# A Strassen-like down product: two half groups of inner tiles, or one over all sixteen

## The chip, the cores and the metric

The kernel runs on one core of a Trainium2 chip. The metric is the device time of one execution in microseconds, and the number compared is the median of several runs.

## The reference

A trunk of two layers on 512 tokens of width 1024. Each layer is a SwiGLU half step, a token mixing (three kinds of attention with gates), and a second SwiGLU half step, with RMS norms before and after each:

```
def _swiglu(t, w_gate, w_up, w_down):
    return (jax.nn.silu(t @ w_gate) * (t @ w_up)) @ w_down

for l in range(DEPTH):
    f = _swiglu(_rmsnorm(h, ffn1_pre_g[l]), ffn1_w_gate[l], ffn1_w_up[l], ffn1_w_down[l])
    h = h + 0.5 * _rmsnorm(f, ffn1_post_g[l])
    ...                                        # token mixing
    f = _swiglu(_rmsnorm(h, ffn2_pre_g[l]), ffn2_w_gate[l], ffn2_w_up[l], ffn2_w_down[l])
    h = h + 0.5 * _rmsnorm(f, ffn2_post_g[l])
```

The inner width D_FF is 2816, that is 22 tiles of 128. So there are four SwiGLUs in a run. Their names in the kernel are a0, c0, a1 and c1; the profile leaves the digit out, so that pda stands for the down product's banks in a0 and a1, and pdc for those in c0 and c1.

## The kernel before

All products run in a split float32 form. Each operand x is cast by ScalarE to a rounded high part (`split`, line 179), VectorE takes the difference as the low part (line 180), and `mm3` (lines 205 to 207) issues three matmuls: high by high, high by low, low by high. In the down product the names of the parts are wh_da and wl_da for the weights, aha and ala for the left factor.

In each SwiGLU the first 16 of the 22 inner tiles go through a seven-product scheme on blocks of two by two (Strassen's, in Winograd's form). Products 0 and 1 add up to one block of the result; the other products are formed from sums and differences of blocks. For the down product, the 16 inner tiles are taken as two half groups of 8 tiles (`ci` 0 and 1; FC is 8, NC is 2). Each half group is a two by two scheme of its own: the left factor's blocks are 256 tokens by 4 inner tiles, the weight's blocks are 4 inner tiles by 512 columns. One product (ci, n) has 4 inner tiles, two tiles of 128 tokens (`e`), and three matmuls each, so 24 matmuls of 512 columns. The last 6 inner tiles (16 to 21) are done plainly: their gate and up columns come in pairs of tiles (18 and 20 here), and `down` multiplies them at the end.

The order of the jobs is written out by hand. `PLAN` (lines 1636 to 1642) weaves the down products, two at a time, between half jobs of the gate and up columns: ("g", 18, 0) is the first half of gate pair 18 (one tile of the pair, 24 matmuls) and ("g", 18, 1) the second; both use the same weights, which are loaded for the first and freed by the second. A `Queue` holds the jobs. When a job begins, the units (weight blocks) of the following jobs are loaded ahead, at least four of them. A unit is fetched by SyncE into a ring buffer ("raw" or "o"), then split into a wh and a wl buffer. The compiler's scheduler then sets the order on each engine.

The buffers that matter, by tag (line 101): four wh and four wl (split weights), two raw and, for the down product, two of the eight o buffers as the fetching ring; further o buffers hold kept weight blocks ("bt", two for each half group, needed from product 2 to product 6) and the hidden tiles 18 to 21; six v buffers hold the left factor's high and low parts and its running sum ("as", from product 2 to product 5); two "k" and two "tri" buffers hold the hidden rows (hr). Four PSUM banks have the tag z.

`products` makes the units of a half group and yields its seven jobs. `product` runs one: it makes the next product's left factor (`first_factor`), opens banks for products 0, 1 and 2, runs the matmuls, and evicts. Product 3, 5 and 6 go on accumulating in the banks of product 0, product 4 in those of product 2 (`SUM`, line 599). `TO` (line 600) says to which quarter of the result a product's bank is evicted, f32 tiles `dst.fs` (fa and fc in the profile). In the first half group, ScalarE copies (lines 875, 878) and VectorE adds (lines 876, 880); in the second half group everything is added by VectorE (line 880), but for product 1's bank, which starts from a ScalarE copy of what is there already (line 856).

`BlockUnit.load` makes the weight's sums and differences with VectorE (line 327). Product 4 uses the raw block of product 3 (`inherits`).

Of the kernel before, what the change touches and what calls it, by code (L numbers as in the profile page):

```python
# [9 lines left out]
F32 = mybir.dt.float32  # L10
# [3 lines left out]
ALU = mybir.AluOpType  # L14
# [3 lines left out]
P = 128  # L18
# [4 lines left out]
def kernel(  # L23
# [38 lines left out]
    nc = tc.nc  # L62
    _, S, D = x.shape
# [11 lines left out]
    FC = 8  # L75
    NC = 2
# [26 lines left out]
    def stile(shape, tag, name, dt=F32R):  # L103
        return sb.tile(shape, dt, tag=tag, bufs=BUFS[tag], name=name)
# [4 lines left out]
    def pbank(tag, name):  # L109
        return ps.tile([P, S], F32, tag=tag, bufs=4, name=name)  # L110
# [65 lines left out]
    def split(h_ap, l_ap, src, scale=None, later=False):  # L176

        if scale is None:
            both = [nc.scalar.copy(h_ap, src)]  # L179
            make = lambda: nc.vector.tensor_tensor(l_ap, src, h_ap.bitcast(F32), ALU.subtract)  # L180
        else:
            both = [nc.scalar.activation(h_ap, src, AF.Copy, scale=scale)]  # L182
            make = lambda: nc.vector.scalar_tensor_tensor(l_ap, src, scale, h_ap.bitcast(F32), ALU.mult, ALU.subtract)  # L183
        if later:
            return make
        both.append(make())
        if Q.pinned:
            for ins in both:
                tc.keep_in_program_order(ins)
# [279 lines left out]
    HF = (slice(0, S), slice(S, D))  # L469
# [129 lines left out]
    SUM = (0, 1, 2, 0, 2, 0, 0)  # L599
# [3 lines left out]
    def ffn(l, src, wg, wu, wd, dst, name, spare, parked, plan, aside=None):  # L603
# [6 lines left out]
        hid, st = {}, {}  # L610
# [116 lines left out]
        def beside(gen, steps, every):  # L727

            for i, us_ in enumerate(gen):
                if i % every == every - 1:  # L730
                    next(steps, None)
                yield us_
# [58 lines left out]
        def turn(tag):  # L791

            nm, g, r = st.pop("turn", (None, None, None))
            if nm is None:
                return
            g = g.rearrange("p f q -> p (f q)")
            for b in range(2):
                pt = pbank(tag, f"ht{nm}_{b}")
                for f in range(2):
                    for e in range(2):  # L800
                        nc.tensor.transpose(pt[:, (2 * f + e) * P:(2 * f + e + 1) * P],
                                            g[:, e * S + (2 * b + f) * P:][:, :P], ident[:])
                nc.scalar.copy(r[:, 2 * b:2 * b + 2], pt[:].rearrange("p (f q) -> p f q", f=2))
                yield 0.4

        def token_products(ci, up):

            w, nm = (wu if up else wg)[l, :, ci * FC * P:(ci + 1) * FC * P], f"{'gu'[up]}{name}_{ci}"
            keep = Keep(lambda k0: stile([P, 2, S], "o", f"t{nm}_{k0}", F32)[:])
            places, had = itertools.cycle(("raw", "o", "o")), {}  # L810
            for n in ORDER:
                uns = [BlockUnit(n, w, ND // 2, k, 2, S, keep, f"{nm}_{n}_{k}", n in (2, 4) or next(places))
                       for k in range(0, ND // 2, 2)]
                if n in (2, 4):
                    for un, of in zip(uns, had[n - 2 + (n == 4)]):
                        un.inherits(of)
                had[n] = uns
                run = lambda n=n, uns=uns: token_product(ci, up, n, uns)
                early = ci == 0 and not up and n in ORDER[:4]
                yield uns, (lambda run=run: beside(run(), itertools.islice(st["some"], 1), 2)) if early else run  # L820
# [4 lines left out]
        def first_factor(ci, n):  # L825

            a = lambda i, j: hr[2 * ci + j][:, :, HALVES[i]]
            nm = f"{name}_{ci}_{n}"
            h, l = (stile([P, FC // 2, S // 2], "v", f"a{x}{nm}")[:] for x in "hl")
            if n == 2:  # L830
                st["s", ci] = stile([P, FC // 2, S // 2], "v", f"as{nm}", F32)[:]
            s = st.get(("s", ci))
            if n == 2:
                nc.vector.tensor_tensor(s, a(1, 0), a(1, 1), ALU.add)
            elif n == 3:
                nc.vector.tensor_tensor(s, s, a(0, 0), ALU.subtract)
            elif n == 4:
                nc.vector.tensor_tensor(s, a(0, 1), s, ALU.subtract)
            elif n == 5:
                nc.vector.tensor_tensor(s, a(0, 0), a(1, 0), ALU.subtract)  # L840
            src = (a(0, 0), a(0, 1), s, s, s, s, a(1, 1))[n]
            split(h, l, src)
            st["a", ci, n] = h, l

        def product(ci, n, uns):
            if n == 0 and ci == 0:
                RINGS["o"] = 2
                dst.begin()
            if n < 6:
                first_factor(ci, n + 1)  # L850
            if n in (0, 1, 2):
                st["b", SUM[n]] = [pbank("z", f"pd{name}_{ci}_{n}_{e}") for e in range(2)]
            pts = st["b", SUM[n]]
            if n == 1 and ci:
                for e in range(2):
                    nc.scalar.copy(pts[e][:], dst.fs[e][:, HF[0]])
            h, l = st["a", ci, n]
            opens, ends = n in (0, 2) or (n == 1 and not ci), n in (1, 4, 6)
            for un in uns:
                for k in range(un.nk):  # L860
                    kk = un.k0 + k
                    for e in range(2):
                        c = slice(e * P, (e + 1) * P)
                        mm3(pts[e][:], h[:, kk, c], l[:, kk, c], un.h[:, k], un.l[:, k], opens and kk == 0,
                            ends and kk == FC // 2 - 1, free=True)
                        yield 3 * S * PE_US
                    if kk == FC // 2 - 2:
                        yield from turn("mm")
            if n == 0:
                return  # L870
            i, hf = TO[n]
            for e in range(2):
                f = dst.fs[2 * i + e][:, HF[hf]]
                if n == 1:
                    nc.scalar.copy(f, st["b", 0][e][:])
                    nc.vector.tensor_tensor(f, f, pts[e][:], ALU.add)
                elif ci == 0 and n in (2, 3, 6):
                    nc.scalar.copy(f, pts[e][:])
                else:
                    nc.vector.tensor_tensor(f, f, pts[e][:], ALU.add)  # L880

        def products(ci):

            keep = Keep(lambda k0: stile([P, 2, S], "o", f"bt{name}_{ci}_{k0}", F32)[:])
            w = wd[l, ci * FC * P:(ci + 1) * FC * P]
            for n in range(7):
                uns = [BlockUnit(n, w, FC // 2, k, 2, S, keep, f"d{name}_{ci}_{n}_{k}", ("raw", "o")[k // 2])
                       for k in range(0, FC // 2, 2)]
                if n == 4:
                    for un, of in zip(uns, had):  # L890
                        un.inherits(of)
                had = uns
                yield uns, (lambda n=n, uns=uns: product(ci, n, uns))

        marks, made = {}, {}

# [15 lines left out]
        def queue(what):  # L912
            kind, n = what[0], what[1]
            if kind in "gu":
                if n not in made:
                    made[n] = plain(n)
                ms = (what[2],) if what[-1] in (0, 1) and len(what) == 3 else range(2)
                uns = made[n][kind == "u"]
                run = (lambda: gates(n, uns, ms)) if kind == "g" else (lambda: ups(n, uns, ms))
                Q.add(uns if ms[0] == 0 else [], run)  # L920
            elif kind == "a":
                Q.add([], lambda: iter(first_factor(n, 0) or ()))
            elif kind == "m":
                if name == "a0":
                    Q.add([], mem_stats)
            else:
                if what not in made:
                    made[what] = products(n) if kind == "d" else token_products(n, kind == "U")
                for one in made[what]:
                    Q.add(*one)  # L930
                    break

        first_pair()
        for what in plan:
            queue(what)
# [698 lines left out]
            yield ("pe", 0.9)  # L1634

    PLAN = 7 * [("G", 0)] + [("m", 0)] + 7 * [("U", 0)] + 7 * [("G", 1)] + 6 * [("U", 1)] + [("a", 0), ("U", 1)]
    downs = iter(6 * [("d", 0)] + [("a", 1), ("d", 0)] + 7 * [("d", 1)])
    for f in (18, 20):
        for kind in "gu":
            for m in range(2):  # L1640
# [57 lines left out]
```

## Time and profile before

| | |
|---|---|
| median of 3 runs | 2399.95 us (2398.45 to 2400.62) |
| the profiled execution | 2400.15 us; span on the core 2398.4 us |
| TensorE, busy share of the span | 99% (11975 matmuls) |
| weight loads (PEld) | 84% |
| VectorE (DVE) | 78% |
| ScalarE (ACT) | 58% |
| granted TensorE clock, mean | 0.997 |
| bytes moved | 338.22 MB, mean 141 GB/s |

Matmuls are pipelined and their ends are modelled, so a share of 99% on TensorE does not yet say that it works at its peak. A row of a group gives the line, engine, operation, output and inputs, the count, then busy us, mean ns of one, and the engine's idle time before it with what ended it.

### The profile page before, as it was taken

Reading aid. Unit: us, or ns where it says so; the run is one execution under the profiler, and the core shown is the slowest. Engines: PE = TensorE matmul, PEld = TensorE weight load, DVE = VectorE, ACT = ScalarE, POOL = GpSimd, SP = SyncE. Lnnn points to the kernel's source line nnn. Section 1 sums busy time; section 2 is a strip of 40 time slices with the busy share of each in tenths; the row PEclk is TensorE's granted clock in tenths of the full one; section 3 lists DMA queues with packets and bytes.
Section 4 is the critical chain, followed back from the end, with each engine's and each line's share of the span. In section 5 each row is a group of like instructions: output and inputs, shape, how many; then the busy total and the mean of one; then the engine's idle time right before and its main releaser. Section 6 shows DMA issues by size and latency. Waiting matters only on the chain.

```text
span 2398.4 us, 31561 instructions
## 1 busy us (share of the span) xinstructions
PE 2375.6 (99%) x11975; PEld 2009.8 (84%) x11975; DVE 1862.4 (78%) x2462; ACT 1392.5 (58%) x2201; POOL 78.4 (3%) x134
## 2 busy tenths in 40 slices
PE   9999999999999999999999999999999999999998
PEld 7788889888888888888888888888888888888887
DVE  8878877577777789788788788766667777887885
ACT  6655565576656555555655554655666664655554
POOL 1000000000111000000000000000001100000000
PEclk9999999999999999999999999999999999999999
DMA  5654454222323555544645554532323235555444
GB/s 200 187 150 158 141 194 140 80 82 78 88 80 99 192 181 170 150 150 158 210 138 170 149 175 162 188 107 71 97 71 97 71 122 191 164 182 149 154 139 155
DMA packets 232171, 338.22 MB, mean 141 GB/s; under 512 B 10682, under 2 KB 125394, under 8 KB 232020
## 3 DMA queue, kind: packets, MB, share of 16 engines
q1 hardware_dynamic: 231924, 336.18, 44.3%
q8 instruction: 94, 1.54, 0.3%
q14 instruction: 57, 0.47, 0.1%
q0 software_dynamic: 96, 0.03, 0.0%
HBM read 319.39 MB, written 16.78 MB: 140 GB/s over the span
## 4 chain that ended last, share of the span: by engine, by line
PE 94%; DVE 3%; DMA 1%; ACT 1%; issue 1%; POOL 0%; DVEq 0%; SPq 0%; ACTq 0%
PE pg L206 4%; PE pg L205 4%; PE pg L207 4%; PE pda L206 3%; PE pda L207 3%; PE pda L205 3%; PE pdc L206 3%; PE pdc L207 2%; PE pdc L205 2%; PE pb L207 2%; PE pb L206 2%; PE pb L205 2%; PE pk L205 1%; PE pk L206 1%; PE pk L207 1%; PE pwo L206 1%
## 5 line engine op out<-in xcount | busy, mean ns | idle before, releaser
L205 PE MATMUL pg<-us_a,wh_wg 128*128 128x512 f32 x384 | 150.8, 393 | 0.0
L206 PE MATMUL pg<-us_a,wh_wg 128*128 128x512 f32 x384 | 149.6, 390 | 0.0
L207 PE MATMUL pg<-us_a,wl_wg 128*128 128x512 f32 x384 | 149.6, 390 | 0.0
L206 PE MATMUL pdc<-wl_dc,ahc 128*128 128x512 f32 x224 | 87.6, 391 | 0.1
L206 PE MATMUL pda<-wl_da,aha 128*128 128x512 f32 x224 | 87.6, 391 | 0.0
L205 PE MATMUL pda<-wh_da,aha 128*128 128x512 f32 x224 | 87.4, 390 | 0.0
L205 PE MATMUL pdc<-wh_dc,ahc 128*128 128x512 f32 x224 | 87.4, 390 | 0.0
L207 PE MATMUL pdc<-wh_dc,alc 128*128 128x512 f32 x224 | 87.2, 389 | 0.0
L207 PE MATMUL pda<-wh_da,ala 128*128 128x512 f32 x224 | 87.2, 389 | 0.0
L207 PEld LDWEIGHTS pg<-us_a,wl_wg 128*128 128x128 f32 x384 | 72.1, 188 | 15.2
L205 PEld LDWEIGHTS pg<-us_a,wh_wg 128*128 128x128 f32 x384 | 72.1, 188 | 14.1
L206 PEld LDWEIGHTS pg<-us_a,wh_wg 128*128 128x128 f32 x384 | 72.2, 188 | 14.0
L180 DVE TENSOR_TENSOR wl_dc<-raw_dc,wh_dc 128x1024 fp32r<-128x1024 f32 x50 | 61.2, 1224 | 29.1 <-ACT wh_dc L179 28.5
L180 DVE TENSOR_TENSOR wl_da<-raw_da,wh_da 128x1024 fp32r<-128x1024 f32 x50 | 61.2, 1224 | 22.0 <-ACT wh_da L179 21.7
L179 ACT CAST wh_dc<-raw_dc 128x1024 fp32r<-128x1024 f32 x50 | 52.7, 1054 | 43.8 <-PE pdc L207 14.9
L179 ACT CAST wh_da<-raw_da 128x1024 fp32r<-128x1024 f32 x50 | 52.7, 1054 | 38.7 <-PE pda L207 14.5
L183 DVE SCALAR_TENSOR_TENSOR wl_wg<-raw_wg,wh_wg 128x1024 fp32r<-128x1024 f32 x48 | 58.4, 1221 | 20.4 <-ACT wh_wg L182 20.1
L179 ACT CAST wh_uc<-raw_uc 128x1024 fp32r<-128x1024 f32 x44 | 46.3, 1053 | 41.9 <-PE pwc1u L207 10.3
L182 ACT ACTIVATE wh_wg<-raw_wg 128x1024 fp32r<-128x1024 f32 x48 | 50.6, 1057 | 28.0 <-PE pv L1089 12.6
L179 ACT CAST wh_ua<-raw_ua 128x1024 fp32r<-128x1024 f32 x44 | 46.2, 1052 | 34.5 <-PE pwa1u L207 10.3
L180 DVE TENSOR_TENSOR wl_uc<-raw_uc,wh_uc 128x1024 fp32r<-128x1024 f32 x44 | 53.7, 1221 | 13.0 <-ACT wh_uc L179 12.9
L180 DVE TENSOR_TENSOR wl_ua<-raw_ua,wh_ua 128x1024 fp32r<-128x1024 f32 x44 | 53.6, 1220 | 10.2 <-ACT wh_ua L179 10.2
(654 smaller groups left out, 8028.8 us busy)
## 6 DMA issues: line engine op xcount, KB each, us to landing
raw_da<-in_ffn_w_down_dram SPq DMA_DIRECT2D x66, 512.0 KB, 4.5
raw_dc<-in_ffn_w_down_dram SPq DMA_DIRECT2D x66, 512.0 KB, 4.9
raw_ga<-in_ffn_w_gate_dram SPq DMA_DIRECT2D x52, 512.0 KB, 3.8
raw_ua<-in_ffn_w_up_dram SPq DMA_DIRECT2D x52, 512.0 KB, 3.9
raw_gc<-in_ffn_w_gate_dram SPq DMA_DIRECT2D x52, 512.0 KB, 3.7
raw_uc<-in_ffn_w_up_dram SPq DMA_DIRECT2D x52, 512.0 KB, 3.7
raw_wg<-in_w_gate_dram SPq DMA_DIRECT2D x48, 512.0 KB, 3.5
raw_wo<-in_w_out_dram SPq DMA_DIRECT2D x24, 512.0 KB, 3.6
```

The source lines that it names most:

```text
L179: both = [nc.scalar.copy(h_ap, src)]
L180: make = lambda: nc.vector.tensor_tensor(l_ap, src, h_ap.bitcast(F32), ALU.subtract)
L182: both = [nc.scalar.activation(h_ap, src, AF.Copy, scale=scale)]
L183: make = lambda: nc.vector.scalar_tensor_tensor(l_ap, src, scale, h_ap.bitcast(F32), ALU.mult, ALU.subtract)
L205: nc.tensor.matmul(pt, lh, rh, start=start, stop=False, skip_group_check=free)
L206: nc.tensor.matmul(pt, lh, rl, start=False, stop=False, skip_group_check=free)
L207: nc.tensor.matmul(pt, ll, rh, start=False, stop=stop, skip_group_check=free)
```

## The change

The two half groups are merged. One list, `DOWN`, gives the order of all 14 products: for each n both half groups in turn, but products 3 and 4 of one half group stay together, since 4 uses 3's raw block. The banks are opened only in the first half group and evicted only after the second, so each of the seven products accumulates over all sixteen inner tiles in PSUM. After product (1,0) the second bank starts from a ScalarE copy of the first bank, and product 1 accumulates on it. `products` makes the units of both half groups with two sets of kept blocks. In `PLAN` 14 equal entries take the place of the two groups' entries; the separate job that made the second group's first factor is gone.

```diff
+        DOWN = [(ci, n) for ns in ((0,), (1,), (2,), (3, 4), (5,), (6,)) for ci in range(NC) for n in ns]
+
-        def product(ci, n, uns):
-            if n == 0 and ci == 0:
+        def product(at, uns):
+            ci, n = DOWN[at]
+            first, last = ci == 0, ci == NC - 1
+            if at == 0:
                 RINGS["o"] = 2
                 dst.begin()
-            if n < 6:
-                first_factor(ci, n + 1)
-            if n in (0, 1, 2):
-                st["b", SUM[n]] = [pbank("z", f"pd{name}_{ci}_{n}_{e}") for e in range(2)]
+            if at + 1 < len(DOWN):
+                first_factor(*DOWN[at + 1])
+            if first and n in (0, 2):
+                st["b", SUM[n]] = [pbank("z", f"pd{name}_{n}_{e}") for e in range(2)]
             pts = st["b", SUM[n]]
-            if n == 1 and ci:
-                for e in range(2):
-                    nc.scalar.copy(pts[e][:], dst.fs[e][:, HF[0]])
-            h, l = st["a", ci, n]
-            opens, ends = n in (0, 2) or (n == 1 and not ci), n in (1, 4, 6)
+            h, l = st.pop(("a", ci, n))
+            opens, ends = first and n in (0, 2), last and n in (1, 4, 6)
             for un in uns:
...
+            if not last:
+                return
             if n == 0:
+                st["b", 1] = [pbank("z", f"pd{name}_1_{e}") for e in range(2)]
+                for e in range(2):
+                    nc.scalar.copy(st["b", 1][e][:], pts[e][:])
                 return
             i, hf = TO[n]
             for e in range(2):
                 f = dst.fs[2 * i + e][:, HF[hf]]
-                if n == 1:
-                    nc.scalar.copy(f, st["b", 0][e][:])
+                if n in (4, 5):
                     nc.vector.tensor_tensor(f, f, pts[e][:], ALU.add)
-                elif ci == 0 and n in (2, 3, 6):
+                else:
                     nc.scalar.copy(f, pts[e][:])
-                else:
-                    nc.vector.tensor_tensor(f, f, pts[e][:], ALU.add)
...
+        def products():
+            keep = [Keep(lambda k0, ci=ci: stile([P, 2, S], "o", f"bt{name}_{ci}_{k0}", F32)[:]) for ci in range(NC)]
+            had = {}
+            for at, (ci, n) in enumerate(DOWN):
+                w = wd[l, ci * FC * P:(ci + 1) * FC * P]
+                uns = [BlockUnit(n, w, FC // 2, k, 2, S, keep[ci], f"d{name}_{ci}_{n}_{k}", ("raw", "o")[k // 2])
                        for k in range(0, FC // 2, 2)]
                 if n == 4:
-                    for un, of in zip(uns, had):
+                    for un, of in zip(uns, had[ci, 3]):
                         un.inherits(of)
...
-    downs = iter(6 * [("d", 0)] + [("a", 1), ("d", 0)] + 7 * [("d", 1)])
+    downs = iter(14 * [("d", 0)])
```

More of the change, by code (lines that the diff above doesn't have):

```diff
@@ L873, in product @@
                 f = dst.fs[2 * i + e][:, HF[hf]]
-                if n == 1:
-                    nc.scalar.copy(f, st["b", 0][e][:])
+                if n in (4, 5):
                     nc.vector.tensor_tensor(f, f, pts[e][:], ALU.add)
-                elif ci == 0 and n in (2, 3, 6):
+                else:
                     nc.scalar.copy(f, pts[e][:])
-                else:
[L880 to L887, printed above, removed]
+        def products():
[4 more added lines that the diff above has]
+                uns = [BlockUnit(n, w, FC // 2, k, 2, S, keep[ci], f"d{name}_{ci}_{n}_{k}", ("raw", "o")[k // 2])
                        for k in range(0, FC // 2, 2)]
                 if n == 4:
-                    for un, of in zip(uns, had):
+                    for un, of in zip(uns, had[ci, 3]):
                         un.inherits(of)
-                had = uns
-                yield uns, (lambda n=n, uns=uns: product(ci, n, uns))
+                had[ci, n] = uns
+                yield uns, (lambda at=at, uns=uns: product(at, uns))
         marks, made = {}, {}
@@ L927, in queue @@
                 if what not in made:
-                    made[what] = products(n) if kind == "d" else token_products(n, kind == "U")
+                    made[what] = products() if kind == "d" else token_products(n, kind == "U")
                 for one in made[what]:
```

## The prediction

> **What bounds the kernel now.** I read the page's first part, then its chain, then TensorE's own waits, then the four stretches in which the changed code runs.
>
> ```profile
> span 2398.4 us, 31561 instructions
> PE 2375.6 (99%) x11975; PEld 2009.8 (84%) x11975; DVE 1862.4 (78%) x2462; ACT 1392.5 (58%) x2201; POOL 78.4 (3%) x134
> ...
> PE 94%; DVE 3%; DMA 1%; ACT 1%; issue 1%; POOL 0%; DVEq 0%; SPq 0%; ACTq 0%
> ```
>
> TensorE is busy for 99% of the span, and 94% of the chain that ended last is its work. "Busy" is modelled for matmuls, so I look for idle time instead. The view of waits, for TensorE (engine, line, what it waited for: us in total, times, longest):
>
> ```profile
> PE pfl L1283 <- DVE fl L1334: 9.0, 2, 4.5
> PE warm L1558 <- DVE warm L1650: 1.3, 1, 1.3
> PE pwa0g L207 <- DVE ula L180: 1.1, 1, 1.1
> ...
> PE pga L654 <- ACT w_ga L179: 0.2, 1, 0.2
> ```
>
> These are four of thirteen rows. None of the thirteen names pda or pdc, the banks of the down product. The four stretches with these products (one for each SwiGLU), by windows:
>
> ```profile
> core 0: us, PE busy (x) PEld busy (x) DVE busy (x) ACT busy (x) POOL busy (x), PEclk, DMA share, GB/s
> 200.20:321.40 121.20, 121.20 (x538) 99.72 (x536) 100.44 (x99) 61.76 (x72) 0.00 (x0) 1.00 0.55 182
> ...
> sum 485.60, PE 485.52 PEld 400.19 DVE 398.94 ACT 248.23 POOL 0.00; mean PE 121.38 PEld 100.05 DVE 99.73 ACT 62.06 POOL 0.00
> ```
>
> In such a stretch stand 14 products and 8 half jobs of the gate and up columns (18 to 21) that the plan weaves between them, each of 24 matmuls. TensorE is busy for 121.20 of 121.20 us, at full clock (1.00); 121.20 over 22 jobs is 5.5 us a job (the 8 transposes at the start are in it). VectorE is busy for 100.44 us, 83%, ScalarE for half, the DMA engines for 55%. So this stage is TensorE's, and taking work off VectorE saves time only where VectorE's lateness is seen by TensorE. Where that is, the weight loads show, in the views of the tiles pda and pdc (what their engine waited for: us, times):
>
> ```profile
>   DVE wl_da L180: 1.3, 4
> ...
>   DVE wl_dc L180: 1.4, 4
> ```
>
> Eight waits, 2.7 us in all, two in each stretch. One of them, from the timeline (start, us, engine, operation, and in brackets the idle time before):
>
> ```profile
> 217.63 0.39 PE L205 MATMUL pda<-wh_da,aha 128*128 128x512 f32 x1
> 217.86 0.39 PE L206 MATMUL pda<-wl_da,aha 128*128 128x512 f32 x1
> 219.92 2.35 DVE L327 TENSOR_TENSOR raw_da<-bta,raw_da 128x1024 f32<-128x1024 f32 x2
> 220.59 1.06 ACT L179 CAST wh_da<-bta 128x1024 fp32r<-128x1024 f32 x1 [2.17 <-PE pda L207]
> 222.19 1.22 DVE L180 TENSOR_TENSOR wl_da<-bta,wh_da 128x1024 fp32r<-128x1024 f32 x1
> 223.46 0.19 PEld L206 LDWEIGHTS pda<-wl_da,aha 128*128 128x128 f32 x1 [0.42 <-DVE wl_da L180]
> ```
>
> At 217.63 product 2 of the first half group starts; at about 223.1, 24 matmuls later, product 3. Weights lie in four wh and four wl buffers. Between the two halves of a gate (or up) pair, its own weights hold two of each, so the products in between share the other two. Product 3's first split must wait until product 2 has used its first pair of tiles: ScalarE waits for TensorE until 220.59, casts for 1.06 us, VectorE comes to it at 222.19, after the block sums of 219.92, and is done at 223.41; the load of the low part runs at 223.46. That is the second product between the two halves of a gate: (0,3) and (1,3) here, which is twice per stretch, as counted. This is the only place where the stage touches TensorE.
>
> **The change part by part.**
>
> *What goes.* The evictions of the second half group, and what joined the groups:
>
> ```profile
> L880 DVE TENSOR_TENSOR fa<-fa,pda x28: 679/681/687, 239.4 to 1506.1; 128x512 f32<-128x512 f32 x28
> L878 ACT COPY fa<-pda x12: 576/585/589, 222.6 to 1447.1; 128x512 f32<-128x512 f32 x12
> L875 ACT COPY fa<-pda x8: 572/584/589, 206.3 to 1457.9; 128x512 f32<-128x512 f32 x8
> L876 DVE TENSOR_TENSOR fa<-fa,pda x8: 680/684/689, 211.7 to 1465.7; 128x512 f32<-128x512 f32 x8
> ...
> L856 ACT COPY pda<-fa 128x512 f32<-128x512 f32 x2 | 1.2, 579 | 0.0
> ```
>
> Counts for pda cover two stretches (L856: one), pdc is the same. VectorE has 14 + 4 = 18 additions in a stretch now, and keeps 4 (products 4 and 5): 14 go, 14 x 0.681 = 9.5 us a stretch, 38 us in all. ScalarE has 6 + 4 + 2 = 12 copies and keeps 10 (two from the first bank into the second, and eight evictions): 2 x 0.58 = 1.2 us a stretch. TensorE keeps every matmul, 14 x 24 a stretch. On the path: nothing. No row says that TensorE waited for an eviction; each bank is next used after at least one other job of 5.5 us, which covers two evictions (2 x 0.68). VectorE falls from 100.4 to 90.9 of 121.2 us.
>
> *What is added: one wait.* The second bank now gets its start by two ScalarE copies out of the first, after product (1,0) has ended; 2 x 0.58 = 1.2 us. The half gate job of 5.5 us lies between (1,0) and (0,1), which needs that bank: cost nothing; without that cover 1.2 us x 4 = 4.7 us. Queued behind these copies on ScalarE are the casts of weights for (0,1) and (1,1), with a job's time to spare.
>
> *What moves: the order.* Two products stand between jobs as before, but now they are (0,0)(1,0), gate 18 first half, (0,1)(1,1), gate 18 second half, (0,2)(1,2), up 18 first half, (0,3)(0,4), up 18 second half, (1,3)(1,4), gate 20 first half, (0,5)(1,5), gate 20 second half, (0,6)(1,6), up 20. The pairs that stand between two halves are now (0,1)(1,1), (0,3)(0,4) and (0,5)(1,5): three second products per stretch, (1,1), (0,4), (1,5), where there were two. (Before, up 18 and up 20 had a single product between their halves, which shares its buffers with nobody.) So 12 waits instead of 8. The trace does not show the new three. From below each is 0 (product 4 has its block in place from product 3, and 1 takes it raw, so neither stands behind a block sum as 3 does): then the 2.7 us are gained. From above each stands behind one more whole VectorE instruction:
>
> ```profile
> L180 DVE TENSOR_TENSOR ala<-asa,aha 128x1024 fp32r<-128x1024 f32 x16 | 19.5, 1221 | 2.5 <-PE pda L206 2.4
> ```
>
> 12 x 1.22 = 14.7 us, less the 2.7 that go: +12.0 us. I take today's mean, 2.7 / 8 = 0.34 us: 12 x 0.34 = 4.05, so +1.35 us. It is the nearest row, the same wait of the same weights.
>
> *Buffers.* Two running sums of the left factor live at once instead of one: with two factors' high and low parts that fills the six v buffers exactly, where one was spare. A factor for the next product can then be split only when the product before the present one has ended. In each pair the second product's factor has a half job and the first product in front of it, some 11 us, for at most three instructions (sum, cast, low part, about 3.5 us): nothing, and up to 1 us for each of 14 if VectorE is late. Four kept weight blocks live at once instead of two; with two ring buffers and the first two hidden tiles they fill the eight o buffers: nothing.
>
> *Transfers.* They are the same in number and size, but product 2's doubled loads now come twice in a row: 8 x 0.512 MB = 4.2 MB, at the stage's 182 GB/s 23 us. They start when (0,1)'s raw blocks have been split, during (1,0), and (1,2) starts five jobs later, 27 us. Hidden, with little to spare at that rate; product 3 and 5 now wait for a raw buffer that a gate's split frees a little over two jobs ahead, as product 2 did before with twice the bytes, and product 2 shows no wait on TensorE. The rows for transfers in section 6 give 4.5 us to landing:
>
> ```profile
> raw_da<-in_ffn_w_down_dram SPq DMA_DIRECT2D x66, 512.0 KB, 4.5
> ```
>
> *The sum.* Evictions 0, the new copy 0, order +1.35, buffers 0, transfers 0: +1.35 us. The profiled execution took 2400.15 us (span 2398.4 and 1.75 around it), so its like would take 2401.5; it lies 0.2 us above the median of the three runs, 2399.95, so I say **2401.3 us**. About 0.2%, 4.8 us, is what a measurement of this kernel can tell from no change, so this is "the same".
>
> **A rule against the row.** The weight loads' groups (busy us, mean ns, idle before them):
>
> ```profile
> L205 PEld LDWEIGHTS pg<-us_a,wh_wg 128*128 128x128 f32 x384 | 72.1, 188 | 14.1
> ...
> L206 PEld LDWEIGHTS pda<-wl_da,aha 128*128 128x128 f32 x224 | 42.1, 188 | 9.9 <-DVE wl_da L180 1.3
> ...
> L205 PEld LDWEIGHTS pda<-wh_da,aha 128*128 128x128 f32 x224 | 42.0, 188 | 8.8
> ```
>
> Before each load lie 8.8 us / 224 = 39 ns in the down product and 14.1 / 384 = 37 ns in the mixing gates, where nothing of this kind is evicted. So the 39 ns belong to the load itself, and only the 1.3 us with a releaser can be won. The Trainium skill, "Perfetto Trace Analysis", section "Identifying the Most-Contended Engine", says that matmul occupancy does not measure the distance to the roofline, and that the busy share of LDWEIGHTS does. By that rule the stage is at 100.05 of 121.38 us, and up to 4 x 21.3 = 85 us could still go; by the rows the sum stays at +1.35 us.
>
> **The rivals.**
>
> *Slower, VectorE late at the twelve places.* In (1,5) the block sums and the sum of the left factor stand ahead of the low part, as in the lines shown. If the fixed order of VectorE's queue puts one more 1.22 us instruction ahead at all of them, +12.0 us: 2412. It decides from a mean wait of (4.8 + 2.7) / 12 = 0.63 us, about twice today's. For it: VectorE still at 75%, four of the heavy products, (0,5)(1,5)(0,6)(1,6), now in a row. Against it: 9.5 us less work, and (1,1) and (0,4) need no block sum. 0.16.
>
> *Slower, SyncE's queue.* One transfer held back the others while it waited for a v buffer:
>
> ```profile
> SPq L1026 <- PE pda L207: 5.2, 1, 5.2
> ```
>
> That cost nothing. If fuller buffers bring one such wait into each stretch, and half of it reaches TensorE, 4 x 2.6 = +10.4 us: 2410. 0.07.
>
> *A little faster.* All waits go: 2399.95 - 2.7 = 2397.25, which is still within 0.2%. 0.08.
>
> *Clearly faster.* Either the stage has room after all: the 1.3 + 1.4 us are all that its own rows give, so this would need the 38 us of VectorE to be on the path, 2362: 0.02. (The rule of the Trainium skill above is on the side of this rival; the equal 37 and 39 ns speak against it.) Or the order of VectorE's queue shifts further on, and the 9.0 us of waits for fl go: 2391, 0.07; nothing in the change touches that code.
>
> That the change doesn't do what it says is not open: the additions are plainly gone from the code.
>
> **How the numbers follow.** Forecast 0.60, and the little gain 0.08, give "same" 0.68; slower 0.16 + 0.07 = 0.23; faster 0.02 + 0.07 = 0.09. The likeliest case by itself runs from 2397 to 2403. The range reaches up to just under the first slower rival, 2411, and down past the little gain by the spread of the runs, to 2396: left out are the clear gain, 0.09, and the upper part of the slower rivals, about 0.08.
>
> **What would show it.** The additions of line 880 fall from 56 to 16, VectorE's busy time in a stretch from 100 to about 91 us, and TensorE's stays at 121. The waits of weight loads for wl_da and wl_dc become 12, at (1,1), (0,4) and (1,5), with some 4 us in sum. No row of TensorE's waits names pd, fa or fc. Wrong would be: a wait of TensorE for ScalarE's copies into the second bank, for the left factor's low part, or for weights that a transfer brought late; or a stretch that is over 1 us longer than 121.4 us.

## The result and the profile after

The merged kernel takes 2407.91 us (median of 6 runs, 2407.06 to 2409.55) against 2400.28 us for the kernel before (6 runs, 2398.12 to 2400.86): 7.6 us more, ratio 1.0035 with a 95% interval of 1.0022 to 1.0048. That is slower by more than the 0.2% of the prediction, and inside its range.

First the page and the chain of waits of the kernel after:

```profile
span 2405.3 us, 31523 instructions
PE 2377.2 (99%) x11975; PEld 2009.5 (84%) x11975; DVE 1828.1 (76%) x2406; ACT 1387.5 (58%) x2193; POOL 78.3 (3%) x134
...
PE 88%; DVE 5%; DMA 4%; ACT 2%; issue 1%; DVEq 0%; SPq 0%; ACTq 0%
```

VectorE has 56 instructions and 34 us less, ScalarE 8 copies less, TensorE the same 11975 matmuls. But TensorE's part of the chain fell from 94% to 88%; VectorE and the DMA engines, which were at 3% and 1%, have 5% and 4%. TensorE's view of waits has two new rows for the down products, directly under the old first one:

```profile
PE pfl L1287 <- DVE fl L1338: 8.7, 2, 4.4
PE pda L206 <- DVE wl_da L180: 3.5, 4, 1.5
PE pdc L206 <- DVE wl_dc L180: 1.6, 2, 0.8
```

The four down stretches (windows; columns as before):

```profile
200.10:322.87 122.77, 121.34 (x537) 99.40 (x535) 91.57 (x85) 60.17 (x69) 0.00 (x0) 1.00 0.49 167
1049.00:1171.30 122.30, 121.52 (x538) 99.54 (x537) 90.29 (x83) 61.21 (x70) 0.00 (x0) 1.00 0.51 168
```

In the first, VectorE is busy for 91.57 us, where it was 100.44; TensorE now has 1.4 us idle in its 122.77. The weight loads of the down product tell it best (groups: busy us, mean ns, idle before them and what ended it):

```profile
L206 PEld LDWEIGHTS pda<-wl_da,aha 128*128 128x128 f32 x224 | 42.0, 188 | 15.3 <-DVE wl_da L180 6.8
L206 PEld LDWEIGHTS pdc<-wl_dc,ahc 128*128 128x128 f32 x224 | 42.0, 188 | 13.0 <-DVE wl_dc L180 4.6
```

They waited 6.8 + 4.6 = 11.4 us for the low parts of weights, where it was 2.7: 8.7 us more, against 7.6 us more in the time. (A load starts ahead of its matmul, so TensorE loses a little less than its loads wait. Most matmuls here start 227 ns after the one before; what the starts lie apart beyond that comes to 9.2 us in the four stretches, against 1.6 us before.) These waits are at (1,1), (0,4) and (1,5) in each stretch and nowhere else in it, sixteen in all, since (1,5) waits for both halves of its weights. They are unlike in size: (0,4) waits 0.34 us each time, 1.4 us in all, (1,1) has 2.7 us, and (1,5) has 7.3 us. One of the longest, at (1,5) in the first stretch, in the timeline of VectorE, ScalarE and the matmuls:

```profile
285.13 1.22 DVE L327 TENSOR_TENSOR bta<-raw_da,bta 128x1024 f32<-128x1024 f32 x1
286.53 1.06 ACT L179 CAST wh_da<-raw_da 128x1024 fp32r<-128x1024 f32 x1 [2.17 <-PE pda L207]
286.77 1.23 DVE L327 TENSOR_TENSOR bta<-raw_da,bta 128x1024 f32<-128x1024 f32 x1 [0.41 <-DMA raw_da<-in_ffn_w_down_dram]
287.91 1.22 DVE L180 TENSOR_TENSOR ala<-hra,aha 128x1024 fp32r<-128x1024 f32 x1
289.05 1.22 DVE L180 TENSOR_TENSOR wl_da<-raw_da,wh_da 128x1024 fp32r<-128x1024 f32 x1
290.32 0.50 PE L206 MATMUL pda<-wl_da,aha 128*128 128x512 f32 x1 [0.93 <-DVE wl_da L180]
```

ScalarE has the high part ready at 287.59. VectorE's low part starts at 289.05, since three instructions stand ahead of it in its queue: both block sums of (0,6), the second held up by its transfer, and the low part of (0,6)'s left factor. None of them is needed before the second half of gate 20 and (1,5) itself are through. At (1,1) it is the same with the block sums of product 2:

```profile
223.00 1.23 DVE L327 TENSOR_TENSOR bta<-bta,raw_da 128x1024 f32<-128x1024 f32 x1 [0.45 <-DMA raw_da<-in_ffn_w_down_dram]
224.14 1.22 DVE L180 TENSOR_TENSOR ala<-asa,aha 128x1024 fp32r<-128x1024 f32 x1
225.28 1.22 DVE L180 TENSOR_TENSOR wl_da<-raw_da,wh_da 128x1024 fp32r<-128x1024 f32 x1
...
226.55 0.50 PE L206 MATMUL pda<-wl_da,aha 128*128 128x512 f32 x1 [0.50 <-DVE wl_da L180]
```

So the theory after the result has two parts. The place: a second product between the two halves of a gate has only two free weight buffers, and its weights can be made only just in time. The queue: how long TensorE waits there is set by what stands ahead of the low part in VectorE's queue. The rival is that merging itself costs: both running sums and four kept blocks fill the buffers, product 2's doubled loads come in a row, and weights are late wherever the products stand.

### The profile page after: what moved, and what is told of

It reads as the page before. It is cut to its first block, busy times and chain, and to the rows that moved or that the text cites. A ratio compares the mean times of both kernels' runs of the same rounds, so it can differ in the third digit from the quotient of the medians.

```text
span 2405.3 us, 31523 instructions
## 1 busy us (share of the span) xinstructions
PE 2377.2 (99%) x11975; PEld 2009.5 (84%) x11975; DVE 1828.1 (76%) x2406; ACT 1387.5 (58%) x2193; POOL 78.3 (3%) x134
## 4 chain that ended last, share of the span: by engine, by line
PE 88%; DVE 5%; DMA 4%; ACT 2%; issue 1%; DVEq 0%; SPq 0%; ACTq 0%
PE pg L205 4%; PE pg L207 4%; PE pg L206 4%; PE pda L206 2%; PE pdc L206 2%; PE pdc L207 2%; PE pda L207 2%; PE pdc L205 2%; PE pda L205 2%; PE pb L207 2%; PE pb L206 2%; PE pb L205 2%; DMA raw_da<-in_ffn_w_down_dram 2%; PE pk L206 1%; PE pk L205 1%; PE pk L207 1%
```

## The experiments

Times are medians; each kernel is compared with the runs of the kernel before on the same chip (2400.28 us for the kernel after; 2400.73 for a_single, b_single, a_alone15 and b_third; 2400.37 for a_order, a_no26, a_best and a_evict; 2400.60 for a_best2 and b_single2).

| run | us | ratio to before, 95% interval | loads' wait for wl, us | TensorE's gaps, us |
|---|---|---|---|---|
| after | 2407.91 | 1.0035 (1.0022 to 1.0048) | 11.4 | 9.2 |
| a_single | 2404.09 | 1.0013 (1.0004 to 1.0022) | 0 | 4.8 |
| b_single | 2399.01 | 0.9992 (0.9983 to 1.0001) | 0 | 0 |
| a_alone15 | 2402.85 | 1.0010 (1.0001 to 1.0019) | 5.3 | 4.1 |
| b_third | 2400.66 | 1.0001 (0.9992 to 1.0010) | 3.0 | 1.9 |
| a_order | 2401.75 | 1.0007 (0.9998 to 1.0016) | 4.2 | 2.5 |
| a_no26 | 2401.36 | 1.0003 (0.9995 to 1.0012) | 4.2 | 2.5 |
| a_best | 2399.61 | 0.9998 (0.9989 to 1.0007) | 0 | 0.3 |
| a_evict | 2404.24 | 1.0018 (1.0009 to 1.0026) | 1.4 | 4.7 |
| a_best2 | 2400.24 | 0.9997 (0.9988 to 1.0006) | 0 | 0.3 |
| b_single2 | 2399.76 | 0.9993 (0.9984 to 1.0002) | 0 | 0 |

The fourth column is the sum of the two weight load groups' waits for wl_da and wl_dc. The last is what the starts of TensorE's matmuls lie apart beyond 227 ns, added up over the four stretches from the timelines (1.6 us in the kernel before). In every row the gaps, less these 1.6 us, agree with the difference in time to the kernel before within 1 us, so the differences between these kernels arise in the down stretches.

**Is it the place?** In the plans below a product is written as its two digits (half group, product), and a half job as kind, pair and half. In the kernel the products of the merged version are all `("d", 0)` and follow `DOWN`. a_single:

```diff
-    00 10 g18.0 01 11 g18.1 02 12 u18.0 03 04 u18.1 13 14 g20.0 05 15 g20.1 06 16 u20.0 u20.1
+    00 10 g18.0 01 g18.1 11 02 u18.0 12 u18.1 03 04 13 g20.0 14 g20.1 05 15 06 u20.0 16 u20.1
```

> The merged kernel, with the plan rewritten so that only one product stands between the two halves of a gate or up pair; the ten others stand before the first half, after the second half, in runs of two or three. Place theory (TensorE waits where a second product stands between two halves, since only two of the four weight buffers are free there): no such place is left, no wait of a weight load for wl_da or wl_dc above 0.3 us, time some 2.7 us under the kernel before, 2396.5 to 2399. Merge theory (the lost 7.6 us come from the merging itself: both running sums and four kept blocks live at once, doubled loads of product 2 in a row, so that weights are late wherever the products stand): still 2405 to 2409, with the waits moved to other products.

2404.09 us: half right. All waits for weights are gone, as the place has it and the merge rival has not. But TensorE got a new one, which I had not seen in my own plan (its view of waits; the two rows make up 3.0 us of the 3.4 us over the kernel before):

```profile
PE pda L205 <- DVE fa L881: 2.0, 2, 1.1
...
PE pdc L205 <- DVE fc L881: 1.0, 2, 0.6
```

In the timeline of the matmuls, at (0,6):

```profile
300.92 0.50 PE L205 MATMUL pda<-wh_da,aha 128*128 128x512 f32 x1 [0.93 <-DVE fa L881]
```

(0,6) stands right behind (1,5) there and adds on to the bank that VectorE has still to evict. So the prediction's sentence that each eviction is covered by another job held for the merged kernel's own plan, and this is the price without the cover.

b_single is the same in the kernel before:

```diff
-    00 01 g18.0 02 03 g18.1 04 05 u18.0 a 06 u18.1 10 11 g20.0 12 13 g20.1 14 15 u20.0 16 u20.1
+    00 01 g18.0 02 g18.1 03 04 u18.0 05 u18.1 06 a 10 11 g20.0 12 g20.1 13 14 15 u20.0 16 u20.1
```

> The kernel before, with the same rewriting of the plan: single products between halves. Place theory: its eight waits (2.7 us) go, 2396.5 to 2399, and the difference to the merged kernel with single products is under 1 us either way, since the evictions cost TensorE nothing. Merge theory says nothing of this kernel: 2400.3 as before.

2399.01 us, at the upper edge of what the place theory says, and no load waits for wl: its eight waits are gone. The time is lower by 1.7 us, though the interval just takes in no change.

a_alone15 moves one product of the merged kernel:

```diff
-    ... 13 14 g20.0 05 15 g20.1 06 16 u20.0 u20.1
+    ... 13 14 05 g20.0 15 g20.1 06 16 u20.0 u20.1
```

> The merged kernel with one product moved: (0,5) goes ahead of the first half of gate 20, so that (1,5) stands alone between its halves; (1,1) and (0,4) stay second products. Place theory: the waits at (1,5), some 5.3 us of TensorE's time in the four stretches, go, those at (1,1) and (0,4) stay: 2402 to 2404. Merge theory: the weights of (1,5) or (0,6) are as late as before, 2406 to 2409.

2402.85 us, as the place has it. No wait is left at (1,5), with the same buffers, sums and loads; those at (1,1) stay (up to 1.3 us) and at (0,4) too.

The waits at (1,1) also show what sets their size. VectorE works in the same order there in all four stretches of this kernel and of the merged one: ahead of the low part stand a block sum of (1,2) and the low part of (0,2)'s left factor. What differs is how long that block sum waits for its transfer. In the second stretch, first the merged kernel, then a_alone15 (block sum, and the load that waited):

```profile
1071.51 1.22 DVE L327 TENSOR_TENSOR btc<-btc,raw_dc 128x1024 f32<-128x1024 f32 x1
1075.06 0.19 PEld L206 LDWEIGHTS pdc<-wl_dc,ahc 128*128 128x128 f32 x1 [0.38 <-DVE wl_dc L180]
...
1071.95 1.23 DVE L327 TENSOR_TENSOR btc<-btc,raw_dc 128x1024 f32<-128x1024 f32 x1 [0.84 <-DMA raw_dc<-in_ffn_w_down_dram]
1075.50 0.19 PEld L206 LDWEIGHTS pdc<-wl_dc,ahc 128*128 128x128 f32 x1 [1.31 <-DVE wl_dc L180]
```

Of the eight waits at (1,1) in the two kernels, five have a block sum that waited for its transfer, 0.32 to 0.84 us, and the load waited 0.47 us longer than that each time. In the other three the block sum waited for nothing, and the load waited 0.38 to 0.48 us.

b_third adds a place to the kernel before:

```diff
-    ... u18.0 a 06 u18.1 10 11 g20.0 12 13 g20.1 14 15 u20.0 16 u20.1
+    ... u18.0 a 06 10 u18.1 11 g20.0 12 13 g20.1 14 15 u20.0 16 u20.1
```

> The kernel before with a third second product between halves: (1,0) joins (0,6) between the halves of up 18; all else in its order. Place theory: one new wait per stretch at (1,0), 0.3 us each or a little more, so +1 to +2 us: 2401.3 to 2402.3, twelve waits. Rival (what counts is merging, or how heavy the run of products is, not the place): no change, 2400.3.

2400.66 us, no change: a miss of the place theory. The waits are the old ones, at (0,3) and (1,3); (1,0), at the new place, waits for nothing. In the first stretch VectorE stands idle there until the cast is done, and the low part is ready at 255.42, just before (1,0) starts at 255.59:

```profile
254.20 1.22 DVE L180 TENSOR_TENSOR wl_da<-raw_da,wh_da 128x1024 fp32r<-128x1024 f32 x1 [1.78 <-ACT wh_da L179]
```

So the place alone does not make a wait. That left the queue.

**Is it VectorE's queue?** a_order changes neither plan nor work. It ties the block sums of (0,2) and (0,6) behind the low part that was loaded before them (`Q.low`), by an order on VectorE without a semaphore:

```diff
+        Q.low = both[-1]
...
+                prev = Q.low
                 ins = nc.vector.tensor_tensor(src, a, b, ALU.subtract)
+                if self.behind:
+                    tc.add_manual_dep(ins.ins if hasattr(ins, "ins") else ins, (prev.ins if hasattr(prev, "ins") else prev).name,
+                                      mybir.DependencyInfo(mybir.DependencyClass.NoSync, mybir.DependencyReason.DATA),
+                                      reason="behind")
...
+                for un in uns:
+                    un.behind = ci == 0 and n in (2, 6)
```

> The merged kernel with its plan and its work unchanged; only in VectorE's queue the block sums of product 2 and of product 6 in the first half group are held behind the low parts of the two units loaded before them, so that they no longer stand ahead of the low parts of (1,1) and (1,5). Theory of the queue (at a place with two free weight buffers TensorE waits as long as VectorE's queue has block sums ahead of the low part, some of them waiting for a transfer): the waits at (1,1) and (1,5) fall from 0.1 to 1.6 us to 0.3 or less, TensorE's stalls in the four stretches from 9.3 to 2 to 4 us, time 2401 to 2403. Theory of the place alone (a second product between halves waits whatever VectorE does): 2407 to 2409. Theory of late weights (the raw blocks of (1,5) land late because buffers are full): 2406 to 2409.

The order of VectorE's instructions in the built programs, the merged kernel on the left, at (1,5):

```
wl_da_0_5_2                          wl_da_0_5_2
raw_da_1_5_0  (block sum)            raw_da_1_5_0  (block sum)
ala_1_5                              ala_1_5
bta_0_0       (block sum of 06)      ala_0_6
bta_0_2       (block sum of 06)      wl_da_1_5_0
ala_0_6                              ala_1_6
wl_da_1_5_0                          wl_da_1_5_2
bta_1_0       (block sum of 16)      bta_0_0       (block sum of 06)
```

(One eviction of fa between the first two lines is left out in both.) 2401.75 us: 6.2 us less than the merged kernel. In its timeline VectorE now stands ready at the first half of (1,5)'s weights and waits for the cast, where the finished cast waited for it:

```profile
286.09 1.23 DVE L180 TENSOR_TENSOR wl_da<-raw_da,wh_da 128x1024 fp32r<-128x1024 f32 x1 [1.32 <-ACT wh_da L179]
```

In its groups the loads' waits are down to 2.1 + 2.1 us:

```profile
L207 PEld LDWEIGHTS pda<-wl_da,aha 128*128 128x128 f32 x224 | 42.0, 188 | 10.6 <-DVE wl_da L180 2.1
...
L207 PEld LDWEIGHTS pdc<-wl_dc,ahc 128*128 128x128 f32 x224 | 42.0, 188 | 10.6 <-DVE wl_dc L180 2.1
```

These are twelve waits of 0.34 to 0.39 us, one at each place, all at the second half of the product's weights. Even they are not what the place itself takes, for parts of later left factors still stand ahead there. At (1,5) the cast for ala_1_6 goes before the weights' second cast on ScalarE, and ala_1_6 before wl_da_1_5_2 on VectorE:

```profile
287.45 1.05 ACT L179 CAST aha<-hra 128x1024 fp32r<-128x1024 f32 x1 [1.40 <-PE pda L207]
288.54 1.22 DVE L180 TENSOR_TENSOR ala<-hra,aha 128x1024 fp32r<-128x1024 f32 x1 [1.23 <-ACT aha L179]
289.69 1.22 DVE L180 TENSOR_TENSOR wl_da<-raw_da,wh_da 128x1024 fp32r<-128x1024 f32 x1
290.95 0.19 PEld L207 LDWEIGHTS pda<-wl_da,aha 128*128 128x128 f32 x1 [0.34 <-DVE wl_da L180]
```

Raw blocks that land late would have shown here too; they don't.

a_no26 takes block sums away instead of moving them, those of products 2 and 6 in both half groups (so its result is not that of the other kernels):

```diff
-            if self.n in (2, 3, 5, 6):
+            if self.name[0] != "d" and self.n in (2, 6) or self.n in (3, 5):
```

> The merged kernel without the block sums of products 2 and 6 in the down product's weights (the kept blocks are used as they are; their transfers stay). Theory of the queue: nothing heavy stands ahead of the low parts of (1,1) and (1,5), so the waits there go to 0.3 or less and the time to 2400.5 to 2402.5. Theory of the place alone: 2407 to 2409. Theory of late transfers: no change at (1,5), 2406 to 2409.

2401.36 us, and the same 2.1 + 2.1 us of waits. Moved or removed, it comes to the same: the block sums ahead of the low parts were the cost.

**Does VectorE's relief, or the merging, matter at all?** a_evict puts back twelve of the fourteen additions a stretch that the merging took from VectorE:

```diff
+            for e in range(2):
+                if not last and n:
+                    nc.vector.tensor_tensor(tmp(f"xe{name}_{n}_{e}")[:], src.us[0][:, 0, 0, :].bitcast(F32), pts[e][:], ALU.add)
             if not last:
                 return
```

> The merged kernel with twelve more VectorE additions from the banks in each stretch (128 x 512, into a scratch tile, after each product 1 to 6 of the first half group), as many as the kernel before had there; they add nothing to the result. If evictions on VectorE cost TensorE nothing, as the prediction had it: 2407 to 2409. If the 0.68 us each of them takes from a queue that is already late at the twelve places: up to 12 x 0.7 us more, 2410 to 2416.

(The kernel before had six VectorE additions in its first half group and twelve in its second, so "as many as the kernel before had there" holds for the second.) 2404.24 us: both expectations missed, it is 3.7 us faster than the merged kernel, although that has less work. The loads wait only 0.7 + 0.7 us for weights, and TensorE has a wait on the new additions instead (its view of waits):

```profile
PE pda L205 <- DVE xea L872: 1.6, 2, 1.2
```

The added instructions changed the orders on the engines as well (at (1,1) the low part of (0,2)'s left factor, which stood ahead of the low part of the weights, stands behind it). Which part of the 3.7 us comes from that order and which from the bank that TensorE now waits for first was not taken apart; the run says that the number of VectorE's instructions is not what counts, not more.

a_best is a_single with a half job between (1,5) and (0,6):

```diff
-    00 10 g18.0 01 g18.1 11 02 u18.0 12 u18.1 03 04 13 g20.0 14 g20.1 05 15 06 u20.0 16 u20.1
+    00 10 g18.0 01 g18.1 11 02 u18.0 12 u18.1 03 04 g20.0 13 g20.1 14 05 15 u20.0 06 u20.1 16
```

> The merged kernel with single products between the halves and with (0,6) no longer right behind (1,5): (0,6) stands between the halves of up 20, (1,6) after them. Theory: in the run with single products before, what was left was TensorE's wait at (0,6) for the eviction of product 5 from the same bank; with half a job in between it goes too, and no stall above 0.1 us is left in the stretches: 2398 to 2399.5, as the kernel before with single products (2399.0), since the evictions that the merging saves are worth nothing. Rival (the merging costs time of its own, by full buffers): 2401 or more.

2399.61 us, 0.1 us above the expected range, with no wait for weights and none for the evictions: with full buffers, doubled loads and all, merging costs nothing that these runs show. To see whether it brings anything, both kernels without places ran on one chip:

> The merged kernel in the order without places, once more, on the same chip as the kernel before in the order without places: no stall in the down stages of either, so the only difference is the merging itself (56 VectorE additions and 8 ScalarE copies fewer). If VectorE's relief is worth nothing to TensorE: the two medians within 1 us, both 0.5 to 2 us under the kernel before. If the relief is worth something: this one is lower by 1 us or more.

> The kernel before in the order without places (single products between halves), for the comparison: 2398.5 to 2399.5, within 1 us of the merged kernel without places if evictions are worth nothing.

2400.24 and 2399.76 us: 0.5 us apart, and not in favour of the merged one; the intervals overlap almost wholly. So the 38 us of additions are worth nothing that these runs can tell. (In one detail each missed its expectation: the merged one lies 0.4 us under the kernel before, where 0.5 to 2 us was expected, and the other 0.3 us above its range.) Both lie under the kernel before (2400.60) by less than their intervals can tell, and b_single, lower by 1.7 and 0.8 us in its two runs, is the lowest version found.

## Why the prediction was right and wrong

- *Evictions on the path: nothing.* Right: 56 additions went (2462 to 2406 instructions), VectorE fell to 91 us in a stretch as worked out, and b_single2 beside a_best2 shows 0.5 us, not 38.
- *The copy into the second bank: nothing.* Right: no wait of TensorE for it in the kernel after.
- *The order adds places, 8 to 12.* Right in the places: (1,1), (0,4), (1,5), in each stretch, and nothing else in the stage; but they have sixteen waits, not twelve. a_order, which has this plan without the block sums of (0,2) and (0,6) ahead, has twelve waits of 4.2 us in sum (4.05 were worked out) and takes 1.4 us more than the kernel before (1.35 were worked out, and the interval takes in no change). That it comes so near is luck in part: those waits are behind left factors, and the row that the price came from is one behind block sums.
- *The price of a wait, 0.34 us: this is the term that failed.* It was 11.4 / 12 = 0.95 us a place. It held at (0,4), 0.34, and nearly at (1,1) in two stretches, 0.38; in the other two (1,1) had 0.92 and 1.05, and (1,5) had 1.5 to 2.5 in each. I carried over the mean of other products' waits, as the nearest row. That row was itself set by what stood ahead in VectorE's queue, so it could not be carried to a new order. The block sums in the lines shown, `raw_da<-bta,raw_da`, are already those of a product behind: only product 5 writes its sum into the raw block. The forecast went with it: 2401.3 against 2407.9.
- *The rival "VectorE late at the twelve places", 2412, 0.16.* This is what happened, though not at all twelve: its deciding point was a mean of 0.63 us, and the mean was 0.95, by (1,5) and half of (1,1). But my argument against it, that (1,1) needs no block sum, was wrong in kind. Not the product's own block sums count but those of the products behind it, which have the transfers to wait for, and which the queue had put ahead.
- *Buffers, transfers and the SyncE queue.* Right that they cost nothing by themselves (a_best, a_no26). The transfers take part in one way that I did not price: a block sum that waits for its transfer holds VectorE and all that stands behind it, and at (1,1) this made the difference between 0.38 and 1.05 us.
- *What would show it.* VectorE's busy time and the additions came as listed there (line 880, now 881, has 16). The signs against it came too: two rows of TensorE's waits name pda and pdc, and the first stretch takes 122.77 us, 1.4 us over 121.4.
- *The rule on weight loads.* The Trainium skill, "Perfetto Trace Analysis", section "Identifying the Most-Contended Engine", takes the busy share of LDWEIGHTS, besides the share of the peak FLOP/s, for the distance to the roofline. Its share is 84% in the kernel before, in the kernel after, and in b_single, which has no wait of its loads left in the stage: in this kernel it did not tell the three apart, and the idle time with a releaser did.

## What to carry to other kernels

Where a buffer comes free just in time, the wait of the busy engine is set by what stands ahead in the queue of the engine that refills it, so read that queue's order at these places, and don't carry a mean wait over from another order. If a long instruction stands ahead that is not needed soon, above all one that waits for a transfer, tying it behind the urgent one can be worth more than removing work: 6.2 us here, against nothing for 38 us of additions. Laying out the jobs so that no such place is left was worth 8.3 us to the merged kernel (a_best). Before taking work off an engine, ask which wait of the bounding engine names it.

## What was not expected of the hardware

More VectorE work made the run shorter (a_evict, 2404.24 against 2407.91 us), by a shift of order and of waits that was not fully taken apart. Single instructions and the granted clock (0.996 to 0.998 in all runs) behaved as in the kernel before.
